# The last down stage of both feed-forward parts as two planned seven-product blocks, with the next norm's work in the plan

## The chip, the cores and the metric

The kernel runs on one core of a Trainium2 chip. The metric is the device time of one execution in microseconds, the median of the runs shown. The profile is one further execution, taken by the hardware profiler.

## The reference

One decoder layer of width 2048 for 256 tokens, in float32: a half-step SwiGLU feed-forward (FFN1), a mixer, a second half-step feed-forward (FFN2), and a final RMS norm.

```python
D_MODEL = 2048; SEQ = 256; D_FF = 5632; FFN_RESIDUAL_SCALE = 0.5

def rms_norm(x, gain):
    var = jnp.mean(x * x, axis=-1, keepdims=True)
    return x * lax.rsqrt(var + NORM_EPS) * gain

def swiglu_ffn(x, w_gate, w_up, w_down):
    return (jax.nn.silu(x @ w_gate) * (x @ w_up)) @ w_down

x = x + 0.5 * swiglu_ffn(rms_norm(x, ffn1_norm), ffn1_w_gate, ffn1_w_up, ffn1_w_down)
z = rms_norm(x, mix_norm) @ w_in          # mixer: a linear recurrence and a short convolution
...
x = x + y @ w_out
x = x + 0.5 * swiglu_ffn(rms_norm(x, ffn2_norm), ffn2_w_gate, ffn2_w_up, ffn2_w_down)
out = rms_norm(x, final_norm)
```

## The kernel before

**Tiles.** The tokens lie in two groups of 128 (t = 0, 1), the model's width in four columns of 512 (c = 0 to 3, `CW` = 512), and the 5632 hidden numbers in 11 units of 512. A matrix product is made in three passes from high and low parts: ScalarE (ACT) casts a weight piece to fp32r (`hi_...`), VectorE (DVE) subtracts to get the rest (`lo_...`), and TensorE (PE) adds high by high, low by high and high by low. One product of a unit (128 tokens, 512 hidden numbers, 512 columns) is therefore 12 matmuls of 512 columns: eight rows that read `hi_d` and four that read `lo_d`. The hidden units are turned (transposed on PE, `ph`) and split the same way into `h`.

**Seven-product blocks.** Two units, two columns and two token groups would take eight products. A block of Strassen's kind makes them with seven, p0 to p6, from sums of weight pieces (made by DVE, or by a transfer on the POOL queue that adds to what lies in memory) and sums of hidden units (`hs`). Its four PSUM banks are `ps_d..._a`, `c`, `d` and `e`; bank a ends as the result of group 1 and d as that of group 0 in one column, e and c in the other. Further units go into the same banks as plain products, x00 to x11: x, unit, column (each is two products, one for each t). With two further units a block has 7 + 8 = 15 products.

**Stages.** Each feed-forward has three down stages: units 0 to 2 in the first, 3 to 6 in the middle, 7 to 10 in the last. The middle stage is laid out by `down_stage` with a `Plan`: steps with an engine, a length, the steps they need and a due time. `run` lists them in the order of a small simulation, and that order is kept on the chip. It makes two blocks, on columns 2 and 1 and then 3 and 0, with p and x items in the order of `down_orders`; the turning of the units still open comes behind the block's p4. What the second block owes to the residual `xres` is handed to the next stage.

The first and the last stage are written out by hand in `down(last)`, and the tile framework's scheduler orders their instructions. Both take column 0 by plain products, columns 1 and 2 by `seven` and column 3 by plain products. With four units that is 8 + 15 + 8 = 31 products. In the first stage the block is on the last two units (`us[-2:]`), since ACT has kept exact copies of those (`turned`, made by `exact` when `again` is set); column 0 takes unit 0, then 2, then 1. Unit 1 is turned last.

**The next norm.** `after(c, t)` is called whenever the last stage has updated a column. For FFN1 it is `to_mixer`: squares for the mixer's norm, and `Norm.later(c)` turns the column; columns 0 to 2 are turned in the stage and column 3 in the mixer's first products. For FFN2 it is `last`, with the final norm's squares and gains. `finish` and `close` end the kernel: the group t = 0 is closed first, then t = 1 in two halves of 256 columns with a bank of their own each (`ps_..._last`); `close` squares, takes the root, scales and stores.

## Time and the profile before

| | |
|---|---|
| time, three runs | 1724.46 us median (1724.23 to 1725.42) |
| the profiled execution | 1725.39 us, of which the span is 1723.6 us |
| TensorE's mean granted clock | 0.998 of full speed |
| PE, DVE, ACT busy | 1708.0, 1527.3 and 1097.9 us |
| FFN1's middle and last down stage | 366.77 to 450.48 and 613.95 to 702.16 |
| FFN2's middle and last down stage | 1380.37 to 1464.10 and 1627.54 to 1715.40 |

Starts and lengths in a row of the timeline are in microseconds from the span's start, and then come the engine, the line, the operation, the tile written and those read, the shape and the count; square brackets give the idle time ahead and what ended it. All rows have line 43, since a wrapper records every operation; they are told apart by their tiles.

### The profile page before, as it was taken

How to read it: one execution, taken by the hardware profiler on the slowest of the kernel's cores; microseconds unless marked ns; L12 is line 12 of the kernel's file. 1: busy time of each engine (PE TensorE's matmuls, PEld its weight loads, DVE VectorE, ACT ScalarE, POOL GpSimd, SP SyncE). 2: the span in 40 equal slices, each digit the busy share in tenths (PEclk: the TensorE clock that was granted, in tenths of full speed). 3: DMA queues.
4: the chain of work that ended last, by engine and by line, in shares of the span. 5: the costliest groups of instructions: out<-in, count | busy, mean ns of one | idle time of the engine just before them, and what ended most of it. 6: DMA issues, size and time to landing. Idle time of an engine off the chain costs nothing.

```text
span 1723.6 us, 20401 instructions
## 1 busy us (share of the span) xinstructions
PE 1708.0 (99%) x7913; PEld 1421.1 (82%) x7913; DVE 1527.3 (89%) x1314; ACT 1097.9 (64%) x1348; POOL 50.8 (3%) x84
## 2 busy tenths in 40 slices
PE   9999999999999999999999999999999999999998
PEld 8888888888888888888888888788888888888876
DVE  7989999998999987887897888789899998999976
ACT  7666576665666655667876656566666665666654
POOL 0010000000000000000000000000000000000000
PEclk9999999999999999999999999999999999999999
DMA  8766777769876865755556675675777778877653
GB/s 284 235 215 219 249 233 234 236 207 266 271 226 226 270 194 182 234 182 185 171 196 212 203 253 155 193 248 169 239 262 226 256 244 249 267 226 237 231 182 122
DMA packets 182450, 383.10 MB, mean 222 GB/s; under 512 B 7508, under 2 KB 10448, under 8 KB 177872
## 3 DMA queue, kind: packets, MB, share of 16 engines
q1 hardware_dynamic: 174656, 340.81, 56.4%
q0 software_dynamic: 7520, 39.92, 11.9%
q8 instruction: 62, 1.02, 0.2%
q10 hardware_dynamic: 176, 1.06, 0.1%
q14 instruction: 36, 0.29, 0.1%
HBM read 339.82 MB, written 2.10 MB: 198 GB/s over the span
## 4 chain that ended last, share of the span: by engine, by line
PE 95%; DVE 2%; ACT 1%; DMA 1%; issue 1%; DVEq 0%; ACTq 0%
PE ps_in L43 10%; PE ps_u_a L43 10%; PE ps_g_a L43 10%; PE ps_d L43 9%; PE ps_d_a L43 7%; PE ps_u_c L43 6%; PE ps_g_c L43 6%; PE ps_u_d L43 4%; PE ps_d_c L43 4%; PE ps_g_d L43 4%; PE ps_d_d L43 3%; PE ps_d_e L43 3%; PE ps_u_e L43 3%; PE ps_o L43 3%; PE ps_g_e L43 3%; PE ps_g L43 2%
## 5 line engine op out<-in xcount | busy, mean ns | idle before, releaser
L43 ACT CAST hi_g_p<-raw_g_w 128x1024 fp32r<-128x1024 f32 (+1 forms) x112 | 139.2, 1263 | 93.6 <-DVE raw_g_w L43 31.9
L43 ACT CAST hi_u_p<-raw_u_w 128x1024 fp32r<-128x1024 f32 x112 | 138.2, 1262 | 65.5 <-PE ps_u_a L43 19.3
L43 DVE TENSOR_TENSOR lo_g_p<-raw_g_w,hi_g_p 128x2560 fp32r<-128x2560 f32 (+2 forms) x72 | 159.9, 2228 | 15.1 <-ACT hi_g_p L43 8.9
L43 DVE TENSOR_TENSOR lo_u_p<-raw_u_w,hi_u_p 128x2560 fp32r<-128x2560 f32 (+2 forms) x72 | 159.1, 2228 | 9.1 <-ACT hi_u_p L43 6.6
L43 PE MATMUL ps_in<-xT_nm,hi_in 128*128 128x512 f32 x512 | 122.5, 391 | 0.0
L43 PEld LDWEIGHTS ps_in<-xT_nm,hi_in 128*128 128x128 f32 x512 | 94.1, 188 | 18.8 <-ACT tha L43 0.5
L43 PE MATMUL ps_d<-hi_d,h 128*128 128x512 f32 x440 | 105.4, 391 | 0.0
L43 PEld LDWEIGHTS ps_d<-hi_d,h 128*128 128x128 f32 x440 | 82.0, 188 | 16.8
L43 DVE TENSOR_TENSOR lo_in<-raw_in,hi_in 128x2048 fp32r<-128x2048 f32 x32 | 73.3, 2290 | 20.7 <-ACT hi_in L43 20.4
L43 ACT CAST hi_in<-raw_in 128x1024 fp32r<-128x1024 f32 x64 | 64.2, 1048 | 33.6 <-PE ps_in L43 18.4
L43 ACT CAST hi_d<-raw_d 128x1024 fp32r<-128x1024 f32 x56 | 55.5, 1047 | 39.3 <-PE ps_d_d L43 11.5
L43 ACT CAST hi_d_p<-raw_d_w 128x1024 fp32r<-128x1024 f32 x56 | 56.1, 1047 | 32.2 <-DVE raw_d_w L43 15.8
L43 ACT CAST hi_d_p<-raw_d 128x1024 fp32r<-128x1024 f32 x56 | 56.5, 1046 | 29.3 <-DVE raw_d L43 16.2
L43 DVE TENSOR_TENSOR lo_d_p<-raw_d,hi_d_p 128x2048 fp32r<-128x2048 f32 x28 | 63.6, 2288 | 11.3 <-ACT hi_d_p L43 11.0
L43 DVE TENSOR_TENSOR raw_u_w<-raw_u_w,raw_u_w 128x1024 f32<-128x1024 f32 (+2 forms) x40 | 69.4, 1756 | 2.8 <-DMA raw_u_w<-in_ffn_w_up_dram 1.8
L43 DVE TENSOR_TENSOR raw_g_w<-raw_g_w,raw_g_w 128x1024 f32<-128x1024 f32 (+2 forms) x40 | 69.5, 1754 | 0.6
L43 DVE TENSOR_TENSOR lo_d<-raw_d,hi_d 128x2048 fp32r<-128x2048 f32 x28 | 63.6, 2288 | 6.8 <-ACT hi_d L43 6.8
L43 DVE TENSOR_TENSOR lo_d_p<-raw_d_w,hi_d_p 128x2048 fp32r<-128x2048 f32 (+1 forms) x36 | 64.8, 1813 | 4.1 <-ACT hi_d_p L43 4.0
L43 PEld LDWEIGHTS ps_in<-xT_nm,lo_in 128*128 128x128 f32 x512 | 65.6, 191 | 2.5
L43 PE MATMUL ps_in<-xT_nm,lo_in 128*128 128x256 f32 x512 | 66.4, 283 | 0.0
L43 DVE TENSOR_TENSOR lo_g_x<-raw_g_x,hi_g_x 128x1536 fp32r<-128x1536 f32 x32 | 56.1, 1754 | 4.6 <-ACT hi_g_x L43 4.6
L43 PE MATMUL ps_u_a<-hi_u_p,x 128*128 128x512 f32 x224 | 57.1, 391 | 0.0
(525 smaller groups left out, 4250.9 us busy)
## 6 DMA issues: line engine op xcount, KB each, us to landing
raw_d<-in_ffn_w_down_dram SPq DMA_DIRECT2D x56, 1024.0 KB, 5.2
raw_g_w<-in_ffn_w_gate_dram SPq DMA_DIRECT2D x32, 1024.0 KB, 6.7
raw_u_w<-in_ffn_w_up_dram SPq DMA_DIRECT2D x32, 1024.0 KB, 6.5
raw_in<-in_w_in_dram SPq DMA_DIRECT2D x32, 1024.0 KB, 5.0
raw_g_x<-in_ffn_w_gate_dram SPq DMA_DIRECT2D x32, 768.0 KB, 7.7
raw_u_x<-in_ffn_w_up_dram SPq DMA_DIRECT2D x32, 768.0 KB, 8.6
raw_u<-in_ffn_w_up_dram SPq DMA_DIRECT2D x23, 1024.0 KB, 6.0
raw_g<-in_ffn_w_gate_dram SPq DMA_DIRECT2D x22, 1024.0 KB, 5.2
```

Source lines behind the costliest of these rows:

```text
L43: ins = getattr(self.engine, name)(*args, **kwargs)
```

## The change

Both last stages become calls of `down_stage`. The stage makes two blocks (columns 1 and 0, then 3 and 2), 30 products instead of 31, and every column's updates are steps of the plan, followed by `after`. In FFN1 the squares and the turning of columns 1 and 0 ("n1", "n0") are steps behind p4 of the second block; columns 2 and 3 are turned in the mixer's first products (`defer`). In FFN2 the final norm's squares and gains are steps, and the last product (p1, group 0) is made in two halves of 256 columns in a bank of their own; `finish` closes group 1 first, then group 0 in halves.

`down` is left to the first stage. No exact copies are made by ACT; the block takes units 0 and 1 (m, n), whose exact values DVE sums from the high and low parts (`v`), and column 0 takes units 0, 1, 2 in turn. In each feed-forward the order has 12 fewer 512-column matmuls. DVE's order has 40 more operations of 512 or 1024 elements a partition and 8 fewer of 2048; ACT has 12 more casts of 1024 and POOL 6 more transfers.

```diff
-            def down(last):
-                us = sorted(set(hidden) | {w[0] for w in waiting})
-                m, n = us[-2:] if turned else us[:2]
-                rest = [u for u in us if u not in (m, n)]
+            def down():
+                m, n, *rest = sorted(set(hidden) | {w[0] for w in waiting})
...
-                        wd, c, rest + [n, m] if turned else [m, n] + rest[::-1], hidden.get, f"d{tag}_{m}_{c}", end,
+                        wd, c, [m, n] + rest, hidden.get, f"d{tag}_{m}_{c}", False,
...
-                def exact():
-                    if again:
-                        act.copy(quad(h), pt)
-                        turned[u, t] = quad(h)
...
-                        for u in () if turned else (m, n):
+                        sh, v = {}, {}
+                        for u in (m, n):
                             for t in range(NT):
-                                turned[u, t] = quad(keep(f"hv{tag}_{u}_{t}"))
+                                v[u, t] = quad(keep(f"hv{tag}_{u}_{t}"))
                                 hi, lo = (f32(hidden[u][:, :, o + t * P : o + (t + 1) * P]) for o in (0, S))
-                                dve.tensor_tensor(turned[u, t], hi, lo, op=ALU.add)
+                                dve.tensor_tensor(v[u, t], hi, lo, op=ALU.add)
...
+                    if final is not None and key == units_only[-1]:
+                        def halves(u=u, q=q):
+                            hi, lo = u.tiles["hi"], u.tiles["lo"]
+                            for o in (slice(0, CW // 2), slice(CW // 2, CW)):
+                                final.append(bank(f"ps_{name}_last")[:, : CW // 2])
+                                parts = [(hi[:, j, o], lo[:, j, o]) for j in range(UK)]
+                                multiply([(final[-1], sf[q], True, True)], parts)
...
             down_orders = (
-                ["p0", "p4", "x01", "x11", "p5", "p1", "p6", "x00", "p3", "x10", "p2"],
-                ["p0", "p4", "x01", "p2", "p5", "x11", "p6", "p1", "p3", "x00", "x10"],
...
+                (
+                    ["p0", "p4", "T", "x01", "x11", "p5", "p1", "p6", "x00", "p2", "p3", "x10"],
+                    ["p0", "p4", "n1", "n0", "x01", "p2", "p5", "x11", "p6", "x00", "x10", "p3", "p1"],
+                ),
+                (
+                    ["p0", "p4", "T", "x01", "x11", "p5", "p1", "p6", "x00", "p2", "p3", "x10"],
+                    ["p0", "p4", "p2", "x01", "p5", "x11", "p6", "x00", "p3", "x10", "p1"],
+                ),
...
+                pairs_of = ((CW, 0), (3 * CW, 2 * CW)) if end else ((2 * CW, CW), (3 * CW, 0))
...
-                    down(True)
+                    final = [] if tag == 2 else None
+                    done, _ = down_stage(s + 1, free, ready, tails, later, final)
+                    if tag == 2:
+                        finish(keep, final)
...
+    def to_mixer(plan, c, t=None, z=None):
...
+            plan.add("ACT", 0.65, lambda: nm.squares(c, (t,)), z, due=40.0)
...
+                turn_into(pt, [xres[:, t, i * P : (i + 1) * P] for i in (k, k + 1) for t in range(NT)])
...
+            a = plan.add("PE", 0.45, turn, *held[c])
...
+                b = plan.add("ACT", 0.41, lambda i=i, parts=parts: parts[i][0](), a, due=5.0)
+                plan.add("DVE", 0.42, lambda i=i, parts=parts: parts[i][1](), b, due=8.0)
...
+        squared = plan.add("ACT", 0.65, square, z, due=10.0)
+        plan.add("DVE", 0.65, lambda: dve.scalar_tensor_tensor(xr, xr, -0.5, fin[:, cs], op0=ALU.mult, op1=ALU.mult), squared, due=25.0)
...
+    def finish(keep, halves):
+        y = [keep(f"y_{t}") for t in range(NT)]
+        Engine.pinned = True
+        close(1, y[1], 0, 1)
+        w = CW // 2
+        for h in range(2):
+            xh = xres[:, 0, D - CW + h * w : D - CW + (h + 1) * w]
+            dve.scalar_tensor_tensor(xh, halves[h], 0.5, xh, op0=ALU.mult, op1=ALU.add)
+            close(0, y[0], h, 2)
```

Three places in the order of instructions show what moves. In a row stand the operation, the tile written, those read, the shape and the count. The first place is PE in FFN1's first down stage, behind column 0's products of unit 0; `ph1_1` are the transposes of unit 1, `h1_2` is unit 2, and `ps_d1_1_0_...` is column 0. Before:

```order
L43 MATMUL ph1_1_1_1222<-ident_71,z1_0_844 128x128 x4
L43 MATMUL ph1_1_0_1230<-ident_71,s1_g1_0_625 128x128 x4
L43 MATMUL ps_d1_1_0_0_1188<-hi_d1_1_0_2_1240,h1_2_1136 128x512 x8
L43 MATMUL ps_d1_1_0_1_1189<-hi_d1_1_0_2_1240,h1_2_1136 128x512 x8
L43 MATMUL ps_d1_1_0_0_1188<-lo_d1_1_0_2_1241,h1_2_1136 128x512 x4
L43 MATMUL ps_d1_1_0_1_1189<-lo_d1_1_0_2_1241,h1_2_1136 128x512 x4
L43 MATMUL ps_d1_1_0_0_1188<-hi_d1_1_0_1_1271,h1_1_1221 128x512 x8
```

After, where `ps_d1_0_0_...` is column 0 and `ps_d1_0_a` the bank of p0 of the block:

```order
L43 MATMUL ph1_1_1_1220<-ident_71,z1_0_844 128x128 x4
L43 MATMUL ph1_1_0_1227<-ident_71,s1_g1_0_625 128x128 x4
L43 MATMUL ps_d1_0_a_1322<-hi_d1_0_p0_1338,h1_0_954 128x512 x3
L43 MATMUL ps_d1_0_0_1_1187<-hi_d1_0_0_1_1236,h1_1_1219 128x512
L43 MATMUL ps_d1_0_a_1322<-hi_d1_0_p0_1338,h1_0_954 128x512 x2
L43 MATMUL ps_d1_0_0_0_1186<-hi_d1_0_0_1_1236,h1_1_1219 128x512
L43 MATMUL ps_d1_0_a_1322<-hi_d1_0_p0_1338,h1_0_954 128x512 x3
L43 MATMUL ps_d1_0_a_1322<-lo_d1_0_p0_1339,h1_0_954 128x512 x3
L43 MATMUL ps_d1_0_0_1_1187<-hi_d1_0_0_1_1236,h1_1_1219 128x512 x3
L43 MATMUL ps_d1_0_0_0_1186<-hi_d1_0_0_1_1236,h1_1_1219 128x512 x7
```

Behind the transposes stood unit 2's 24 matmuls, and unit 1 came after them. Now unit 1 (`h1_1`) comes at once, and matmuls of p0 stand between its first ones; unit 2 comes after unit 1.

The second place is the end of FFN2 on PE; `ps_d2_7_3_0` and `_1` are column 3 of the two token groups, `h2_7` to `h2_10` the units. Before:

```order
L43 MATMUL ps_d2_7_3_0_13244<-hi_d2_7_3_8_13310,h2_8_12098 128x512 x8
L43 MATMUL ps_d2_7_3_0_13244<-lo_d2_7_3_8_13311,h2_8_12098 128x512 x4
L43 MATMUL ps_d2_7_3_0_13244<-hi_d2_7_3_7_13317,h2_7_12271 128x512 x8
L43 MATMUL ps_d2_7_3_0_13244<-lo_d2_7_3_7_13318,h2_7_12271 128x512 x4
L43 MATMUL ps_d2_7_3_1_13245<-hi_d2_7_3_8_13310,h2_8_12098 128x512 x8
L43 MATMUL ps_d2_7_3_1_13245<-lo_d2_7_3_8_13311,h2_8_12098 128x512 x4
L43 MATMUL ps_d2_7_3_last_13358<-hi_d2_7_3_7_13317,h2_7_12271 128x256 x8
L43 MATMUL ps_d2_7_3_last_13358<-lo_d2_7_3_7_13318,h2_7_12271 128x256 x4
L43 MATMUL ps_d2_7_3_last_13371<-hi_d2_7_3_7_13317,h2_7_12271 128x256 x8
L43 MATMUL ps_d2_7_3_last_13371<-lo_d2_7_3_7_13318,h2_7_12271 128x256 x4
```

After, where `ps_d2_4_1_a` is group 1 of column 3 and `_d` group 0:

```order
L43 MATMUL ps_d2_4_1_d_13169<-lo_d2_4_1_x00_13298,h2_10_12804 128x512 x4
L43 MATMUL ps_d2_4_1_a_13133<-lo_d2_4_1_x00_13298,h2_10_12804 128x512 x4
L43 MATMUL ps_d2_4_1_a_13133<-hi_d2_4_1_p3_13296,h2_8_12120 128x512 x8
L43 MATMUL ps_d2_4_1_a_13133<-lo_d2_4_1_p3_13335,h2_8_12120 128x512 x4
L43 MATMUL ps_d2_4_1_a_13133<-hi_d2_4_1_x10_13348,h2_9_12869 128x512 x8
L43 MATMUL ps_d2_4_1_d_13169<-hi_d2_4_1_x10_13348,h2_9_12869 128x512 x8
L43 MATMUL ps_d2_4_1_a_13133<-lo_d2_4_1_x10_13370,h2_9_12869 128x512 x4
L43 MATMUL ps_d2_4_1_d_13169<-lo_d2_4_1_x10_13370,h2_9_12869 128x512 x4
L43 MATMUL ps_d2_4_1_last_13398<-hi_d2_4_1_p1_13324,h2_8_12120 128x256 x8
L43 MATMUL ps_d2_4_1_last_13398<-lo_d2_4_1_p1_13353,h2_8_12120 128x256 x4
L43 MATMUL ps_d2_4_1_last_13411<-hi_d2_4_1_p1_13324,h2_8_12120 128x256 x8
L43 MATMUL ps_d2_4_1_last_13411<-lo_d2_4_1_p1_13353,h2_8_12120 128x256 x4
```

The bank of the group that is closed first (`_3_0` before, `_a` now) was complete 12 matmuls of 512 and 24 of 256 columns ahead of the end. It is now complete 4 of 512 and 24 of 256 columns ahead.

The third place is DVE at the same end; `fin` is the final norm's gain, `y` column 3 times that gain, and `fr` the factor of a group. Before:

```order
L43 SCALAR_TENSOR_TENSOR xres_70<-ps_d2_7_3_0_13244,xres_70 128x512
L43 TENSOR_TENSOR y_0_13384<-xres_70,fin_12908 128x512
L43 RECIPROCAL fy_0_0_13392<-fy_0_0_13392 128x1
L43 SCALAR_TENSOR_TENSOR fv_0_0_13391<-part_0_0_13387,pre_0_13229 128x1
L43 SCALAR_TENSOR_TENSOR fq_0_0_13393<-fv_0_0_13391,fy_0_0_13392 128x1
L43 SCALAR_TENSOR_TENSOR fr_0_0_13394<-fq_0_0_13393,fy_0_0_13392 128x1
L43 TENSOR_SCALAR xres_70<-xres_70,fr_0_0_13394 128x256
L43 TENSOR_SCALAR xres_70<-xres_70,fr_0_0_13394 128x640
L43 TENSOR_SCALAR y_0_13384<-y_0_13384,fr_0_0_13394 128x512
L43 SCALAR_TENSOR_TENSOR xres_70<-ps_d2_7_3_1_13245,xres_70 128x512
L43 SCALAR_TENSOR_TENSOR xres_70<-ps_d2_7_3_last_13358,xres_70 128x256
L43 TENSOR_TENSOR y_1_13385<-xres_70,fin_12908 128x256
```

After:

```order
L43 SCALAR_TENSOR_TENSOR xres_70<-ps_d2_4_1_a_13133,xres_70 128x512
L43 SCALAR_TENSOR_TENSOR xres_70<-ps_d2_4_1_d_13169,xres_70 128x512
L43 TENSOR_TENSOR y_1_13427<-xres_70,fin_12781 128x512
L43 RECIPROCAL fy_1_0_13433<-fy_1_0_13433 128x1
L43 SCALAR_TENSOR_TENSOR fv_1_0_13432<-part_1_0_13428,pre_1_13350 128x1
L43 SCALAR_TENSOR_TENSOR fq_1_0_13434<-fv_1_0_13432,fy_1_0_13433 128x1
L43 SCALAR_TENSOR_TENSOR fr_1_0_13435<-fq_1_0_13434,fy_1_0_13433 128x1
L43 TENSOR_SCALAR xres_70<-xres_70,fr_1_0_13435 128x256
L43 TENSOR_SCALAR xres_70<-xres_70,fr_1_0_13435 128x640
L43 TENSOR_SCALAR y_1_13427<-y_1_13427,fr_1_0_13435 128x512
L43 SCALAR_TENSOR_TENSOR xres_70<-ps_d2_4_1_last_13398,xres_70 128x256
L43 TENSOR_TENSOR y_0_13426<-xres_70,fin_12781 128x256
```

Before, one update of 512 (`ps_d2_7_3_0`) led the closing of the first group, and the other group's update and its first half stood behind it. Now two updates (`_a` for group 1, `_d` for group 0) lead it, and only halves stand behind.

More of the change, by code (lines that the diff above doesn't have):

```diff
@@ L1524, in result @@
                         return
-                    for key in keys:
-                        plan.add("DVE", add_ps, lambda key=key: update(c, t, snaps[key]), made[key], due=9.0)
-                    z = plan.add("DVE", add_ps, lambda: update(c, t, ps()), done, due=6.0)
+                    parts = [plan.add("DVE", add_ps, lambda key=key: update(c, t, snaps[key]), made[key], due=9.0) for key in keys]
+                    z = plan.add("DVE", add_ps, lambda: update(c, t, ps()), done, *(parts if then else ()), due=6.0)
                     if then:
@@ L1650, in down_stage @@
                     sevens(
-                        plan, wd, cols, f"d{tag}_{s}_{i}", sh, rows, xs, rooms, orders[i], pairs[11 * i : 11 * i + 11],
-                        down_result(plan, cols, handed if i else None), fills=fills, down=True,
+                        plan, wd, cols, f"d{tag}_{s}_{i}", sh, rows, xs, rooms, [item(z) for z in down_orders[tag if end else 0][i]],
+                        pairs[11 * i : 11 * i + 11],
+                        down_result(plan, cols, handed if i and not end else None, (lambda c, t, z: after(plan, c, t, z)) if end else None),
+                        fills=fills, down=True, final=final if i else None,
                     )
```

157 lines of the change are left out of this document (78 added, 79 removed).

## The prediction

> **What bounds the kernel now.** I read the page first: the busy times, and the chain of work that ended last.
>
> ```profile
> span 1723.6 us, 20401 instructions
> PE 1708.0 (99%) x7913; PEld 1421.1 (82%) x7913; DVE 1527.3 (89%) x1314; ACT 1097.9 (64%) x1348; POOL 50.8 (3%) x84
> PE 95%; DVE 2%; ACT 1%; DMA 1%; issue 1%; DVEq 0%; ACTq 0%
> ```
>
> TensorE (PE) is busy for 99% of the span and carries 95% of the chain. A matmul taken away is therefore time taken away, unless another engine is then late. VectorE (DVE), at 89%, is the one that could be. Next, the waits of PE in the whole span:
>
> ```profile
> PE ps_d_c L43 <- ACT s_d L43: 1.7, 1, 1.7
> PE ps_d_e L43 <- ACT ps_d_c L43: 1.3, 2, 0.7
> ```
>
> The first of these is in FFN2's last down stage, which the change rewrites. The second is a wait of 0.66 in both middle down stages, whose plan the change takes as its pattern. For the price of a matmul I took the longest run of plain ones from the chain:
>
> ```profile
> 186.78 16.32 PE ps_d L43 x72
> ```
>
> So a 512-column matmul takes 16.32/72 = 0.2267 us, and a product of 12 takes 2.72 us. Last, the four stages in question by windows, which I cut at the first matmul of each stage and at the first of what follows: middle and last of FFN1, then middle and last of FFN2. The columns are the stretch, its length, the busy time of PE, PEld, DVE, ACT and POOL, the granted clock, and the DMA.
>
> ```profile
> 366.77:450.48 83.71, 83.05 (x370) 68.37 (x368) 75.07 (x59) 52.45 (x60) 3.47 (x6) 1.00 0.82 249
> 613.95:702.16 88.21, 88.21 (x405) 73.07 (x404) 70.26 (x60) 55.99 (x85) 1.08 (x6) 1.00 0.57 183
> 1380.37:1464.10 83.73, 83.07 (x370) 68.19 (x369) 75.75 (x61) 52.31 (x60) 4.03 (x6) 1.00 0.81 249
> 1627.54:1715.40 87.86, 86.19 (x393) 71.08 (x391) 67.07 (x62) 46.98 (x66) 0.86 (x1) 1.00 0.46 154
> ```
>
> The middle stage is the new last stage measured: two seven-product blocks, each with 15 products, laid out by the same planner. It takes 83.7 us where the last stages take 88.2 and 87.9. Both clocks are at 1.00, so the difference is work and waits.
>
> **FFN1's last stage.** Before, it had 31 products; now it has 30. The order of instructions has 12 fewer 512-column matmuls in each FFN. The rest of the difference is turning (transposes) and waiting:
>
> ```profile
> 414.97 1.89 PE L43 MATMUL ps_d_e<-hi_d_x,h 128*128 128x512 f32 x7 [0.66 <-ACT ps_d_c L43]
> 677.70 3.79 PE L43 MATMUL ps_d<-hi_d,h 128*128 128x512 f32 x16
> 683.14 1.03 PE L43 MATMUL pt_nm<-ident,xres 128*128 128x128 f32 x8
> 683.93 3.89 PE L43 MATMUL ps_d<-hi_d,h 128*128 128x512 f32 x16
> ```
>
> A group of eight transposes costs 683.93 - 683.14 = 0.79. The sixteen matmuls behind it take 0.1 more than the sixteen at 677.70, which have no turning ahead: I take 0.89. The plan puts the turning of columns 1 and 0 (two such groups) behind p4 of the second block, which is just where the middle stage waits 0.66 for the copies of its banks. So I start from 83.71, take off 0.66 and add 2 x 0.88: 84.8. Before, the stage turned three columns of the next norm and the mixer's opening one; now it is two and two, so 0.89 moves over the border into the mixer. The gain is 88.21 - 84.8 - 0.89 = 2.5. Counted the other way, 12 x 0.2267 = 2.7. I keep 2.5, and 2.2 to 2.8 as its bounds.
>
> **FFN2's last stage.** Here the middle stage is the pattern again, with no turning. The last product is split into two halves of 256 columns. The same split stands at the end of the kernel now:
>
> ```profile
> 1709.64 1.98 PE L43 MATMUL ps_d<-hi_d,h 128*128 128x512 f32 x8
> 1712.36 1.12 PE L43 MATMUL ps_d_last<-hi_d,h 128*128 128x256 f32 x8
> 1714.76 0.64 PE L43 MATMUL ps_d_last<-lo_d,h 128*128 128x256 f32 x4
> ```
>
> Both halves take 1714.76 + 0.64 - 1712.36 = 3.04, which is 0.32 over a whole product. So the stage takes 83.73 + 0.32 = 84.05, and the gain is 87.86 - 84.05 = 3.8. In it is one product (2.7), the wait of 1.7 for the sums of hidden units, which the plan doesn't have, and on the other side the pattern's 0.66 and the 0.32. With a wait of up to 1 us more somewhere, the bound is 2.8; without the 0.66 it is 4.5. What could bring such a wait is DVE's load (a rival below) and the POOL transfers that add weight pieces, 40 instead of 34 in the program:
>
> ```profile
> L43 ACT CAST hi_d_p<-raw_d_w 128x1024 fp32r<-128x1024 f32 x56 | 56.1, 1047 | 32.2 <-DVE raw_d_w L43 15.8
> raw_d_w<-raw_d_w POOLq DMA_DIRECT2D x8, 1024.0 KB, 7.3
> ```
>
> A transfer lands 7.3 after its issue. The closest case is the second block's: one raw tile holds the weights of p4, p5 and p3 in turn, so the transfer for p3 starts when p5's low part is done, before PE comes to p5. From there to p3 stand p5, x11 (two products), p6 and x00 (two): six products, 16.3 us. Less two casts of 1.05 and a low part of 2.29 (its row is below), about 12 are left for 7.3. It is hidden.
>
> **The first down stages.** The seven block is now on units 0 and 1 rather than 1 and 2. Unit 1 is turned last, and is now used at once, where before unit 2's 24 matmuls lay behind the turning. The scheduler fills the gap with eleven matmuls of p0. The rows of FFN1 (ACT's copies of the unit turned first, PE's first matmuls behind the turning of unit 1, ACT's casts, DVE's low parts of p0's weights and of the hidden unit), and then of FFN2:
>
> ```profile
> 137.40 1.19 ACT L43 COPY u_g<-ph 128x512 f32<-128x512 f32 x2 [0.39 <-DVE h L43]
> 145.58 3.91 PE L43 MATMUL ps_d<-hi_d,h 128*128 128x512 f32 x16
> 145.79 1.06 ACT L43 CAST h<-ph 128x512 fp32r<-128x512 f32 x2
> 145.94 2.29 DVE L43 TENSOR_TENSOR lo_d_p<-raw_d,hi_d_p 128x2048 fp32r<-128x2048 f32 x1
> 148.14 1.28 DVE L43 TENSOR_TENSOR h<-ph,h 128x512 fp32r<-128x512 f32 x2
> 1158.87 3.89 PE L43 MATMUL ps_d<-hi_d,h 128*128 128x512 f32 x16
> 1158.72 1.08 ACT L43 CAST h<-ph 128x512 fp32r<-128x512 f32 x2 [0.20 <-PE ph L43]
> 1159.02 2.29 DVE L43 TENSOR_TENSOR lo_d_p<-raw_d,hi_d_p 128x2048 fp32r<-128x2048 f32 x1
> ```
>
> In FFN1, unit 1's first matmul is now the fourth behind the turning, at 145.58 + 3 x 0.2267 = 146.26; the first of the two casts ends at about 146.3, a wait of 0.1 at most. The low part of p0's weights is needed by the eleventh, at 145.58 + 10 x 0.2267 = 147.85, and was there at 145.94 + 2.29 = 148.23. It should come earlier, since ACT no longer makes the copies (1.19) ahead of its casts. In FFN2, unit 1's first matmul is the second behind the turning, at 1159.10, and the first cast ends at about 1159.26: 0.2. The eleventh comes at 1161.14, the low part at 1161.31: 0.2 again, as the casts there come behind a transfer. Unit 1's own low parts are needed 19 matmuls behind the turning, at 149.9, and are there at 149.4. The sums that replace the copies put 4 x 0.6 on DVE, two of them ahead of the turning, where DVE is idle now:
>
> ```profile
> 139.02 0.69 DVE L43 TENSOR_TENSOR s_u<-ps_u_d,s_u 128x512 f32<-128x512 f32 x1 [1.06 <-PE ps_u_d L43]
> 1152.84 0.69 DVE L43 TENSOR_TENSOR s_u<-ps_u_d,s_u 128x512 f32<-128x512 f32 x1 [1.08 <-PE ps_u_d L43]
> ```
>
> The 1.2 us of the two sums fits into those 1.06 and 1.08 and what else is idle there. The cost: 0.1 + 0.4 = 0.5. The bounds: 0, and 3.0 if the sums are not absorbed (148.23 + 1.2 - 147.85 = 1.6 and 1161.31 + 1.2 - 1161.14 = 1.4).
>
> **The tail.** DVE's last rows now:
>
> ```profile
> 1709.84 0.69 DVE L43 SCALAR_TENSOR_TENSOR xres<-ps_d,xres 128x512 f32<-128x512 f32 x1 [4.88 <-PE ps_d L43]
> 1710.57 0.69 DVE L43 TENSOR_TENSOR y<-xres,fin 128x512 f32<-128x512 f32 x1
> 1711.71 0.16 DVE L43 RECIPROCAL fy<-fy 128x1 f32<-128x1 f32 x1 [0.45 <-ACT fy L43]
> 1713.54 0.68 DVE L43 SCALAR_TENSOR_TENSOR xres<-ps_d,xres 128x512 f32<-128x512 f32 x1
> 1714.33 0.42 DVE L43 SCALAR_TENSOR_TENSOR xres<-ps_d_last,xres 128x256 f32<-128x256 f32 x1
> 1715.43 0.42 DVE L43 SCALAR_TENSOR_TENSOR xres<-ps_d_last,xres 128x256 f32<-128x256 f32 x1 [0.21 <-PE ps_d_last L43]
> ```
>
> Call E the end of PE's last matmul, 1715.40 now. The first group of tokens to be closed has its sum 5.76 before E (1709.64), and DVE is free in time for the last half, which it takes at E + 0.03. After the change, the bank of the first closed group (a) is done only 3.95 before E: behind it come 4 matmuls on d (0.91) and the halves (3.04). DVE updates from a at E - 3.75 and from d at E - 2.84 (0.20 behind PE, as 1709.84 is behind 1709.64), multiplies y from E - 2.11, starts the reciprocal at E - 1.38, and 1713.54 - 1711.71 = 1.83 later it comes to the first half: E + 0.45. The second half follows 0.89 later (two steps of 0.42 with their gaps), at E + 1.34. Everything from there to the end is the same. The cost is 1.3. It would be 0.5 if the two updates don't stand in a row, and 1.8 if a step of ACT is in the way.
>
> **The sum.** 2.5 + 3.8 - 0.5 - 1.3 = 4.5 us. The profiled execution took 1725.39 (1.8 around its span), 0.9 above the median; I put the sum on the median: 1724.46 - 4.5 = 1720.0. The rest of the program's order is unchanged.
>
> The Trainium skill, "TensorE: Matmul & The Clock Gate", section "Back-to-back issue gap", gives N/2.4 + 2.5 ns for an isolated matmul of N columns, thus an estimate of 216 ns for 512, and by it the 24 matmuls are worth 5.2 us rather than the row's 24 x 0.2267 = 5.4; its sustained 131 ns would make them 3.1, which the row of 72 contradicts.
>
> **The rivals.**
>
> *Sums not absorbed (0.15).* The unit that is turned late makes PE wait 1.6 and 1.4 in the first down stages. Against it: the idle time above. The gain is then 4.5 + 0.5 - 3.0 = 2.0, the time 1722.5: within the 0.2%. A longer wait would cost more than itself, as the one of 2.68 shows, with the granted clock in the eighth column of its window:
>
> ```profile
> 1110.00:1114.00 4.00, 2.17 (x7) 1.69 (x8) 4.00 (x3) 2.00 (x2) 0.86 (x1) 0.82 0.40 80
> 1111.83 1.49 PE L43 MATMUL ps_u_c<-hi_u_p,xs 128*128 128x512 f32 x4 [2.68 <-ACT hi_u_p L43]
> ...
> 1116.95 1.08 PE L43 MATMUL ps_u_c<-lo_u_p,xs 128*128 128x512 f32 x4
> ```
>
> The 15 matmuls from 1111.83 to 1116.95 took 5.12 instead of 3.40: 1.7 lost to the clock. One such wait would bring the time to about 1724. The same page of the Trainium skill, section "What's actually happening", halves the clock after an idle window of about 3.4 us; here a wait of 2.68 was enough. The stages' windows, with waits of 0.66 and 1.66 in them, stay at 1.00.
>
> *A longer tail or seam (0.10).* The closing chain on DVE, or the mixer's first columns with one more group to turn, gives back 2 more: 1722, within the 0.2%.
>
> *DVE becomes the bound (0.13): the one that ends slower.* In the middle stages DVE is busy 75.07 of 83.71 and 75.75 of 83.73, so 8.6 and 8.0 are idle. On top of the pattern, FFN1's last stage gets eight low parts of 0.42 and two updates of 0.69 (4.7), FFN2's gets six scalings of 0.69, a gain of 0.4 and two updates (5.9): 10.6 in all. DVE works in order, and a low part behind a scaling that waits for ACT's square keeps PE waiting. For it: 81.7 of 84 busy leaves 3% idle. Against it: nothing follows FFN2's last stage, so the low parts that the middle stage makes for its successor (2.29 each) fall away, and the last stages before show 70.26 and 67.07. If nothing is absorbed, the time is 1720.0 + 10.6 = 1730.6. It decides from 4.5 unabsorbed, and is outside the 0.2% from 8. I give 0.10 to that and 0.03 to a part of it that ends near 1724.
>
> *The change doesn't do what it says.* Excluded for the work: the order shows the 24 matmuls gone.
>
> **How the numbers follow.** A measurement of this kernel tells 0.2% (3.4 us) from no change: faster is below 1721.0, slower above 1727.9. My forecast, 1720.0, has 0.62. Its own bounds: with first downs at 0, the tail at 0.5 and 2.7 for FFN1 the gain is 6.0 (1718.4), and runs scatter by 0.5: low 1717.9. The range goes up over the first two rivals, and a small wait with them, to 1723.8. Left out above it are DVE as the bound and the wait that lowers the clock. Faster 0.62, same 0.28 (0.15 + 0.10 + 0.03), slower 0.10.
>
> **What would show it.** Right: FFN1's last stage at 84.8 and FFN2's at 84.1 from first to last matmul, without waits of PE over 0.7 in them; waits under 0.4 behind the turning of unit 1; the second half's update 1.3 behind PE's last matmul, and 9.5 from that matmul to the end of the span instead of 8.2. Wrong: waits of PE for low parts (lo_d) in the last stages, DVE above 95% there; waits over 1 us for h in the first down stages; PE idle at the mixer's first matmuls.

## The result, and the profile after

The changed kernel takes 1719.34 us (median of 7 runs, 1718.1 to 1721.4) where the kernel before takes 1725.12 (median of 7, 1722.83 to 1726.03). The ratio is 0.9970, with a 95% interval from 0.9959 to 0.9982: faster by 5.2 us, 3.1 to 7.1. The forecast was 1720.0, a gain of 4.5.

The first lines of the profile page after, then the five longest rows of PE's waits (total, times, longest):

```profile
span 1718.7 us, 20426 instructions
PE 1702.2 (99%) x7889; PEld 1414.9 (82%) x7889; DVE 1549.4 (90%) x1346; ACT 1110.7 (65%) x1360; POOL 56.1 (3%) x90
PE 96%; DVE 2%; DMA 1%; issue 1%; ACT 1%; DVEq 0%; ACTq 0%
```

```profile
PE ps_u_c L43 <- ACT hi_u_p L43: 2.7, 1, 2.7
PE ps_d_e L43 <- ACT ps_d_c L43: 1.3, 2, 0.7
PE idle L43 <- DVE ones L43: 1.1, 1, 1.1
PE ps_d_c L43 <- ACT ps_d_c L43: 0.7, 1, 0.7
PE ps_u_e L43 <- DVE lo_u_x L43: 0.5, 2, 0.3
```

PE's records are 24 fewer and PE is busy 5.8 us less; DVE is busy 22 us more, and PE is still the chain. The wait of 1.7 for sums of hidden units is gone. In its place stands the pattern's 0.66 in FFN2's new block (`ps_d_c`). The last row is new, and it is in FFN2's second gate and up stage, which the change doesn't touch.

The stages by windows, cut as before: FFN1's last stage, the mixer's start (up to the first matmul of `ps_in_c`), FFN2's second gate and up stage, FFN2's last stage. Then the second and third of these from the kernel before, which were not shown yet:

```profile
612.98:697.49 84.51, 84.51 (x386) 70.15 (x384) 78.81 (x72) 63.93 (x93) 2.92 (x9) 1.00 0.76 224
697.49:722.05 24.56, 24.56 (x150) 21.65 (x148) 19.47 (x26) 15.00 (x23) 0.91 (x8) 1.00 0.85 300
1212.78:1378.21 165.43, 164.56 (x734) 135.05 (x732) 154.12 (x99) 104.87 (x102) 6.51 (x8) 1.00 0.73 234
1625.58:1709.60 84.02, 83.36 (x381) 68.94 (x379) 75.90 (x75) 54.96 (x75) 2.71 (x4) 1.00 0.64 188
```

```profile
702.16:725.64 23.48, 23.48 (x142) 20.90 (x140) 18.12 (x23) 13.38 (x20) 0.92 (x8) 1.00 0.74 269
1216.52:1380.27 163.75, 163.75 (x733) 135.22 (x732) 154.37 (x99) 104.96 (x102) 6.37 (x8) 1.00 0.74 236
```

Both new last stages came out as the middle stage had said: 84.51 and 84.02, at a clock of 1.00. With cuts like these, at the first matmul of each part on PE, the two profiled executions can be laid side by side. "First down" runs from the turning of unit 1 to the block's second product (p4), "its block" from there to the first `ps_g_a` of the next stage.

| stretch (us) | before | after | difference |
|---|---|---|---|
| start to the first 16 `ps_g` matmuls in a row | 20.20 | 18.26 | -1.94 |
| FFN1's first down / its block | 14.53 / 43.63 | 15.13 / 43.78 | +0.60 / +0.15 |
| FFN1's last stage | 88.21 | 84.51 | -3.70 |
| mixer's start | 23.48 | 24.56 | +1.08 |
| FFN2's opening, up to the turning | 141.17 | 140.53 | -0.64 |
| FFN2's first down / its block | 14.50 / 43.94 | 15.10 / 43.78 | +0.60 / -0.16 |
| FFN2's second gate and up stage | 163.75 | 165.43 | +1.68 |
| FFN2's last stage | 87.86 | 84.02 | -3.84 |
| PE's last matmul to the end of the span | 8.2 | 9.1 | +0.9 |

The stretches left out differ by 0.4 in sum. The rows that the change writes anew (first downs, last stages, mixer's start, end) add up to about -4.4. The -1.94 at the start is no part of it: over the fourteen profiles of this document, whose kernels start alike, the start takes 18.1 to 18.5 in seven and 19.9 to 20.3 in the other seven. What differs is the pace of the first matmuls, before and then after:

```profile
5.88 2.08 PE L43 MATMUL ps_g<-hi_g,xT_n 128*128 128x512 f32 x4 [0.21 <-ACT hi_g L43]
5.89 1.20 PE L43 MATMUL ps_g<-hi_g,xT_n 128*128 128x512 f32 x4 [0.51 <-ACT hi_g L43]
```

From the second matmul on they follow each other after 0.43 us in the first row and after 0.23 in the second. The seven late profiles all show the slow pace here, the other seven the fast one.

The end, in DVE's rows after:

```profile
1705.86 0.69 DVE L43 SCALAR_TENSOR_TENSOR xres<-ps_d_a,xres 128x512 f32<-128x512 f32 x1 [2.15 <-PE ps_d_a L43]
1706.77 0.69 DVE L43 SCALAR_TENSOR_TENSOR xres<-ps_d_d,xres 128x512 f32<-128x512 f32 x1 [0.21 <-PE ps_d_d L43]
1707.38 0.68 DVE L43 TENSOR_TENSOR y<-xres,fin 128x512 f32<-128x512 f32 x1
1707.97 0.16 DVE L43 RECIPROCAL fy<-fy 128x1 f32<-128x1 f32 x1
...
1709.80 0.42 DVE L43 SCALAR_TENSOR_TENSOR xres<-ps_d_last,xres 128x256 f32<-128x256 f32 x1
1710.25 0.42 DVE L43 TENSOR_TENSOR y<-xres,fin 128x256 f32<-128x256 f32 x1
1710.59 0.42 DVE L43 SCALAR_TENSOR_TENSOR xres<-ps_d_last,xres 128x256 f32<-128x256 f32 x1
```

PE's last matmul ends at E = 1709.60. The update from a starts at E - 3.74 and that from d at E - 2.83, as worked out. The second half is taken at E + 0.99, without idle time ahead of it: DVE is late with it, not PE.

### The profile page after: what moved, and what is told of

Its sections match the earlier page's. It is cut to its first block, busy times and chain, and to the rows that moved or that the text cites. A ratio compares the mean times of both kernels' runs of the same rounds, so it can differ in the third digit from the quotient of the medians.

```text
span 1718.7 us, 20426 instructions
## 1 busy us (share of the span) xinstructions
PE 1702.2 (99%) x7889; PEld 1414.9 (82%) x7889; DVE 1549.4 (90%) x1346; ACT 1110.7 (65%) x1360; POOL 56.1 (3%) x90
## 3 DMA queue, kind: packets, MB, share of 16 engines
q8 instruction: 62, 1.02, 0.2%
q10 hardware_dynamic: 176, 1.06, 0.1%
## 4 chain that ended last, share of the span: by engine, by line
PE 96%; DVE 2%; DMA 1%; issue 1%; ACT 1%; DVEq 0%; ACTq 0%
PE ps_in L43 10%; PE ps_g_a L43 10%; PE ps_u_a L43 10%; PE ps_d_a L43 9%; PE ps_g_c L43 6%; PE ps_u_c L43 6%; PE ps_d_c L43 5%; PE ps_d_d L43 4%; PE ps_d_e L43 4%; PE ps_u_d L43 4%; PE ps_g_d L43 4%; PE ps_d L43 4%; PE ps_o L43 3%; PE ps_g L43 3%; PE ps_u L43 3%; PE ps_g_e L43 3%
## 5 line engine op out<-in xcount | busy, mean ns | idle before, releaser
L43 ACT CAST hi_d_p<-raw_d_w 128x1024 fp32r<-128x1024 f32 x112 | 112.7, 1048 | 54.5 <-DVE raw_d_w L43 23.0
L43 DVE TENSOR_TENSOR lo_d_p<-raw_d_w,hi_d_p 128x2048 fp32r<-128x2048 f32 (+1 forms) x72 | 129.4, 1812 | 5.8 <-ACT hi_d_p L43 5.5
L43 ACT CAST hi_d_x<-raw_d_x 128x1024 fp32r<-128x1024 f32 x64 | 64.3, 1048 | 18.8 <-PE ps_d_c L43 8.3
L43 DVE TENSOR_TENSOR lo_d_x<-raw_d_x,hi_d_x 128x2048 fp32r<-128x2048 f32 x32 | 72.6, 2286 | 1.4 <-ACT hi_d_x L43 1.4
L43 ACT CAST hi_g_x<-raw_g_x 128x1536 fp32r<-128x1536 f32 x32 | 47.2, 1476 | 14.8 <-DMA raw_g_x<-in_ffn_w_gate_dram 11.1
L43 PE MATMUL ps_g_a<-hi_g_p,x 128*128 128x512 f32 x224 | 56.6, 389 | 0.0
L43 DVE TENSOR_TENSOR lo_u_x<-raw_u_x,hi_u_x 128x1536 fp32r<-128x1536 f32 x32 | 56.1, 1752 | 0.0
L43 ACT CAST hi_u_x<-raw_u_x 128x1536 fp32r<-128x1536 f32 x32 | 47.2, 1476 | 12.6 <-PE ps_u_c L43 7.0
```

Of the source, the lines that this page charges most:

```text
L43: ins = getattr(self.engine, name)(*args, **kwargs)
```

## The experiments

Stretches are read from each run's own profiled execution, with the same cuts. The times of two single executions are not set against each other, since the start scatters by 2 us and FFN2's opening by 4; stretches are.

**The parts one by one.** The first kernel has the new first down stages with the old last stages; the second and third have in addition one of the two new last stages each.

```diff
 # e1: both last stages as before; e2: only FFN2's; e3: only FFN1's
-                    done, _ = down_stage(s + 1, free, ready, tails, later, final)
+                    down_last()      # the function down(True) of before
```

> Only the two first down stages are changed (block on units 0 and 1, exact values by DVE's sums, column 0 in the order 0, 1, 2); both last stages are as before. Theory (the late-turned unit costs little): 1.2 us slower than before, 0.6 in each first down stage, of which the profile shows about 0.6 between the turning of unit 1 and the 35th 512-column matmul behind it. Rival (the sums are not absorbed): 3.0 us slower. Rival (nothing is late): no difference, and the 35 matmuls take 35 x 0.2267 = 7.9 us.

> The changed kernel with FFN2's last stage and the closing as before. Theory (the stage pays, the mixer takes back what is moved): 1.4 us faster than before: FFN1's last stage 3.7 shorter at 84.5, the mixer's start 1.1 longer, the first downs 1.2 longer. Rival (the moved turning exposes a wait at the mixer's start and takes all back): 0 to 1 us slower. FFN2's last stage at 87.9 with its wait of 1.7 for sums.

> The changed kernel with FFN1's last stage and the mixer's start as before. Theory: 1.7 us faster than before: FFN2's last stage 3.8 shorter at 84.0, the end 0.9 longer, the first downs 1.2 longer. Rival (the end gives back more, as the second group's halves stand behind the first group's scaling): under 0.5 us faster. FFN1's last stage at 88.2.

| | ratio to before (95%) | first downs | FFN1's last / mixer's start | FFN2's last / end |
|---|---|---|---|---|
| first downs alone | 1.0010 (1.0001 to 1.0018) | 15.06, 15.13 | 88.16 / 23.48 | 87.90 / 8.2 |
| and FFN1's last stage | 0.9992 (0.9984 to 1.0001) | 16.44, 15.13 | 84.50 / 24.57 | 87.70 / 8.2 |
| and FFN2's last stage | 0.9997 (0.9989 to 1.0006) | 14.98, 15.12 | 88.18 / 23.47 | 84.02 / 9.2 |

FFN1's last stage, the mixer's start, FFN2's last stage and the end follow their own edits within 0.2 us, and nothing else. The first downs alone make the kernel slower, by 1.7 us (0.2 to 3.1), where 1.2 was expected. The second is 1.4 faster (2.8 faster to 0.2 slower), as expected. The third is 0.5 faster (1.9 faster to 1.0 slower) where 1.7 was expected: inside the interval, but not shown by it. For the second and third it is the stretches that speak against the rivals, not the times.

**Where the first downs lose.** Two other orders for them. In the first, the block is on units 1 and 2 and the plain columns 0 and 3 take units 0, 2, 1, as before, with the sums still on DVE. In the second the block stays on units 0 and 1.

```diff
-                m, n, *rest = sorted(...)
+                *rest, m, n = sorted(...)                       # e4 only
-                        wd, c, [m, n] + rest, hidden.get, ...
+                        wd, c, rest + [n, m], hidden.get, ...   # e4
+                        wd, c, [m] + rest + [n], hidden.get, ...  # e6
```

> The changed kernel with the first downs' block on units 1 and 2 and column 0 in the order 0, 2, 1 as before; the exact values are still DVE's sums. Theory (the waits come from using the unit that is turned last at once): the 24 matmuls of unit 2 cover the turning again, 1.0 to 1.2 us faster than the changed kernel, about 6 us faster than before. Rival (the sums on DVE are what is late, now behind the turning of both units): no faster than the changed kernel, with waits for hs in the block of the first down stage.

> The changed kernel with its block on units 0 and 1, but column 0 (and 3) of the first down stages takes the units 0, 2, 1, so that unit 2's 24 matmuls lie behind the turning of unit 1 again. Theory (the first downs lose only by using the late unit at once, and the sums for the block are in time): the stretch from the turning to the block's second product 14.5 us as before, instead of 15.1, in both, and the block no longer than 43.8. Rival (the sums of unit 1 come too late for a block that starts 0.6 earlier, as in the run with the block on units 1 and 2): the block is longer by 0.6 or more.

The block on units 1 and 2 is slower than before: ratio 1.0022 (1.0013 to 1.0031). Its waits of PE in the two first downs, by the timeline:

```profile
167.76 0.96 PE L43 MATMUL ps_d_a<-hi_d_p,hs 128*128 128x512 f32 x3 [2.96 <-ACT s_d L43]
1181.39 0.96 PE L43 MATMUL ps_d_a<-hi_d_p,hs 128*128 128x512 f32 x3 [2.92 <-ACT s_d L43]
```

The stretch from the turning to p4 is back at 14.52 and 14.50, but the blocks take 47.07 and 46.97 instead of 43.78: all four exact sums now come behind the turning, and the sums of hidden units are late by 3 us. My theory for that run fell. Units 0 and 1 belong to DVE's sums, since unit 0's can be made early. With that kept and only the order of column 0 put back, the other run has both: PE behind the turning of unit 1, by the timeline of FFN1,

```profile
144.91 0.60 PE L43 MATMUL ph<-ident,s_g 128*128 128x128 f32 x4
145.27 3.89 PE L43 MATMUL ps_d<-hi_d,h 128*128 128x512 f32 x16
148.99 1.98 PE L43 MATMUL ps_d<-lo_d,h 128*128 128x512 f32 x8
```

The stretches are 14.49 and 14.50, and the blocks 43.67 and 43.66. So 0.6 in each first down is the price of using the unit that is turned last at once. With that order FFN1's first down also hangs on when its weights land. In the ten profiles that have it, it took 14.9 to 16.4, and in step with ACT's wait for the transfer: 14.98 with a wait of 0.23, 15.13 with 0.40 (the changed kernel), 15.39 with 0.64, 15.95 with 1.20, 16.44 with 1.72, and 14.9 in the two that list none. In the four with unit 2 behind the turning it took 14.49 to 14.53, also where the wait was 1.28.

**The end.** Three edits of FFN2's last stage and of the closing.

```diff
 # e7: group 1's scaling on ACT and POOL
-        close(1, y[1], 0, 1)
+        rest = close(1, y[1], 0, 1)
+        rest(((act, 0, 640),))
+        rest(((pool, 640, 1536), (pool, 1536, 2048)))
 # e8: columns 2 and 3 swapped, another order
-                    ["p0", "p4", "p2", "x01", "p5", "x11", "p6", "x00", "p3", "x10", "p1"],
+                    ["p0", "p4", "p1", "x01", "p5", "p6", "x00", "p3", "x10", "x11", "p2"],
 # e9: x10 first high and low on bank a, then on d; d's update behind close(1, ...)
                             u.over(to(b), ...)
+                            if split:
+                                u.under((to(b), ...))
```

> The changed kernel with the scaling of the first closed group taken off DVE: ACT takes its first 640 columns and POOL the other 1408. Theory (the halves' updates are late because they stand behind that scaling on DVE): the second half's update starts 0.1 us behind PE's last matmul instead of 1.0, and the end comes 8.2 to 8.4 behind it instead of 9.1. Rival (it is late by the chain of root and factor, or POOL's scaling becomes the last work): 9.1 or more.

With POOL the second half starts at E + 0.35 instead of 0.99, but the end comes 10.0 behind E: the rival. DVE's and POOL's rows of that run:

```profile
1709.77 1.02 DVE L43 TENSOR_TENSOR y<-xres,fin 128x256 f32<-128x256 f32 x1
1711.16 0.42 DVE L43 TENSOR_TENSOR y<-xres,fin 128x256 f32<-128x256 f32 x1
1712.17 0.56 DVE L43 SCALAR_TENSOR_TENSOR fv<-part,pre 128x1 f32<-128x1 f32 x1
1709.51 2.53 POOL L43 TENSOR_SCALAR xres<-xres,fr 128x896 f32<-128x896 f32 x1 [26.26 <-DVE fr L43]
1712.04 1.55 POOL L43 TENSOR_SCALAR y<-y,fr 128x512 f32<-128x512 f32 x1
```

POOL takes 2.53 and 1.55 us, so group 1's last piece is stored only at 1713.62, and group 0's pieces stand behind it in SP's queue. Its last piece is issued at E + 5.14, where the changed kernel has E + 4.86; the rest of the 0.8 that the end is longer is open. And while POOL works, one of DVE's steps of 256 took 1.02 (0.42 after) and a step of one element 0.56 (0.14), each just behind the start of a step of POOL. The same step for the second half, at 1711.16, took 0.42 with POOL still at work.

> The changed kernel with FFN2's last block turned round: columns 2 and 3 swap their places, p1 comes behind p4 (its bank is ready then), and p2 is the halved last product. Theory (the wait of 0.66 behind p4 is only for the copy of its bank): the wait is gone and FFN2's last stage takes 83.4 instead of 84.0. Rival (p1's weights are needed 16 products earlier, and the loads or DVE are then late): new waits for lo_d_p or hi_d, the stage at 84.0 or more.

Nothing won: 84.06. The wait behind p4 is gone, but p6 now comes right behind p5 on bank a and waits for the copy between them:

```profile
1686.24 2.11 PE L43 MATMUL ps_d_a<-hi_d_p,hs 128*128 128x512 f32 x8 [0.71 <-ACT u_d L43]
```

> The changed kernel with FFN2's last plain product (x10) finished on bank a before it starts on bank d, and group 0's update from d made behind the closing of group 1. Bank a is then complete 5.8 us before PE's last matmul, as before, and not 4.0. Theory (the halves are late because group 1's closing starts late): the second half's update starts 0.0 to 0.1 us behind PE's last matmul instead of 1.0, and the end comes 8.2 to 8.3 behind it instead of 9.1. Rival (the low part of x10 is needed 1.8 us earlier and is late): a wait of PE for lo_d_x and FFN2's last stage longer by as much as the end is shorter.

This was right. PE's rows and DVE's of that run:

```profile
1700.77 1.98 PE L43 MATMUL ps_d_a<-hi_d_x,h 128*128 128x512 f32 x8
1702.58 1.07 PE L43 MATMUL ps_d_a<-lo_d_x,h 128*128 128x512 f32 x4
1703.49 1.98 PE L43 MATMUL ps_d_d<-hi_d_x,h 128*128 128x512 f32 x8
```

```profile
1703.69 0.69 DVE L43 SCALAR_TENSOR_TENSOR xres<-ps_d_a,xres 128x512 f32<-128x512 f32 x1 [0.34 <-PE ps_d_a L43]
1707.39 0.68 DVE L43 SCALAR_TENSOR_TENSOR xres<-ps_d_d,xres 128x512 f32<-128x512 f32 x1
1709.28 0.42 DVE L43 SCALAR_TENSOR_TENSOR xres<-ps_d_last,xres 128x256 f32<-128x256 f32 x1 [0.21 <-PE ps_d_last L43]
```

E is 1709.24 here. Bank a is complete at 1703.49, 5.75 ahead; the second half is taken at E + 0.04 with DVE waiting for PE; the end comes 8.2 behind E, and the stage still takes 83.98 without a new wait in it. So the 0.9 is the late start of group 1's closing, and the update from d that stood in its way; the run moves both, and their shares stay open.

**DVE's slack, and what the turning covers.** Twelve further steps of 0.69 on DVE in FFN2's last stage; and the turning of two columns in FFN1's put behind x01.

```diff
+        for _ in range(2):                                                  # e10, 3 columns of 2 groups
+            plan.add("DVE", 0.65, lambda: dve.scalar_tensor_tensor(xr, xr, 1.0, xr, op0=ALU.mult, op1=ALU.max), squared, due=10.0)
-                    ["p0", "p4", "n1", "n0", "x01", "p2", ...
+                    ["p0", "p4", "x01", "n1", "n0", "p2", ...               # e11
```

> The changed kernel with 12 further operations of 0.69 us on DVE in FFN2's last stage (each gives back its own input), 8.3 us of work placed by the same plan. In the changed kernel DVE is busy 75.9 of 84.0 us there, and about 4 of the 8.1 idle lie in the last 6 us. Theory (DVE is not the bound, but has only some 4 us left): the stage gets 3 to 5 us longer, with waits of PE for low parts. Rival (the order of DVE, and not its load, decides, and there is no slack at all): 8 us longer. Rival (DVE is far from mattering): under 1 us longer.

```profile
1624.81:1712.34 87.53, 84.30 (x381) 68.64 (x379) 82.16 (x83) 54.40 (x74) 2.68 (x4) 1.00 0.61 180
1683.61 1.20 PE L43 MATMUL ps_d_a<-hi_d_p,hs 128*128 128x512 f32 x4 [0.70 <-ACT hi_d_p L43]
1686.92 0.74 PE L43 MATMUL ps_d_a<-lo_d_p,hs 128*128 128x512 f32 x2 [1.65 <-DVE lo_d_p L43]
1710.02 0.68 DVE L43 SCALAR_TENSOR_TENSOR xres<-ps_d_a,xres 128x512 f32<-128x512 f32 x1
```

Of 8.3 us the stage lengthens by 3.5 (87.53 against 84.02), with waits for high and low parts in front of p5 and p6. The end lengthens too, to 10.3 from 9.1: DVE comes to the update from a only at E - 2.32 (E is 1712.34) instead of E - 3.74, with no idle time ahead of it. The other 3.6 found room in idle time.

> The changed kernel with the turning of columns 1 and 0 in FFN1's last stage put behind x01 instead of behind p4. Theory (behind p4 the turning covers the wait of 0.66 for the copies of the banks): that wait comes back, and the stage takes 85.1 to 85.2 instead of 84.5. Rival (the wait is hidden anyway): 84.5.

The stage takes 85.48 instead of 84.51, and the wait is there:

```profile
659.46 1.09 PE L43 MATMUL ps_d_e<-lo_d_p,hs 128*128 128x512 f32 x4
661.21 2.11 PE L43 MATMUL ps_d_e<-hi_d_x,h 128*128 128x512 f32 x8 [0.66 <-ACT ps_d_c L43]
663.17 1.99 PE L43 MATMUL ps_d_c<-hi_d_x,h 128*128 128x512 f32 x8
```

The listed 0.66 costs the stage 0.97. Four matmuls behind 659.46 the next could have started, at 659.46 + 4 x 0.2267 = 660.37, so PE paused for some 0.8; the record of the last matmul, 0.39 long where the next can follow after 0.2267, covers 0.16 of it. The eight matmuls behind the pause then take 663.17 - 661.21 = 1.96 instead of 1.81.

**FFN2's gate and up stage.** It has the same instructions before and after, and was 1.68 longer after. One run set the turn of the weight rooms back to what it had been.

```diff
+                    recent["raw"], recent["pair"] = deque((0, 2, 1)), deque((0, 1))
```

> The changed kernel, but behind FFN1's last stage the turn in which the three raw rooms are given out is set to what it was before (0, 2, 1; the change leaves 2, 1, 0). Theory (the 1.2 to 1.7 us that FFN2's second gate and up stage takes longer in every run with the new FFN1 stage come from the rooms that its loads then get): that stretch, 165.4 us in the changed kernel, falls back to 163.8 to 164.3. Rival (it is a matter of when the transfers fall, not of the rooms): it stays at 165.4 or more.

The stretch is 165.39: the rooms are not the cause. In all eleven profiles with FFN1's new last stage it took 164.97 to 165.59, and in the three with the old one (before, and two of the experiments) 163.75 to 164.26. FFN2's opening goes the other way: 138.0 to 140.5 in the eleven, 140.8 to 142.5 in the three. Part of the opening's scatter is the granted clock: behind a wait in it the clock is halved for 3.41 us in eleven of the fourteen profiles, for 6.83 in one (first downs alone, 142.5), and not at all in two (138.0 and 138.4); each 3.41 loses 1.7. Without that loss the two stretches together take 303.3 to 304.3 in the eleven and 303.2 to 303.4 in the three. DVE's row in the changed kernel shows what is late:

```profile
1266.09 2.82 DVE L43 TENSOR_TENSOR raw_u_w<-raw_u_w,raw_u_w 128x2560 f32<-128x2560 f32 x1 [2.50 <-DMA raw_u_w<-in_ffn_w_up_dram]
```

A weight transfer lands later there: this step starts 53.3 us into the stage, where before it started 51.0 into it. Why it does so is open. The opening wins back a part of what this stretch loses, between the two profiles compared above 0.64 of 1.68.

**Both mends together.**

> The changed kernel with both mends together: column 0 of the first downs in the order 0, 2, 1, and bank a complete early at the end. If they add up as single looks showed (1.2 in the first downs, 0.9 at the end), it is 2.1 us faster than the changed kernel, 6.5 us by the sum of the stretches against before (1718.0 where before is 1724.5), and the stretches are 14.5 and 14.5 from the turnings to the blocks, 84.0 for FFN2's last stage and 8.2 for the end. Rival (the time won comes back as later transfers in FFN2's gate and up stages): 1.0 us or less faster than the changed kernel.

| | ratio to before (95%) | first downs and blocks | FFN2's last / end |
|---|---|---|---|
| the change | 0.9970 (0.9959 to 0.9982) | 15.13 + 43.78, 15.10 + 43.78 | 84.02 / 9.1 |
| with both mends | 0.9963 (0.9950 to 0.9977) | 14.53 + 44.54, 14.49 + 43.69 | 84.02 / 8.2 |

The stretches are as expected, but for FFN1's block, where this execution had a wait for a low part of 0.6 and the run with the order alone had none; ACT's wait for the weights' transfer was 1.28 here and 0.30 there. The median of 6 runs is 1719.24 (1716.29 to 1719.45). Against before it is 6.4 us faster; that it beats the change itself is shown for the stretches (0.6 in FFN2's first down, 0.9 at the end) and not by the times, whose intervals overlap. The 2.1 that was expected against the change is not shown, and the rival (1.0 or less) is not excluded.

## Why the prediction was right

- *What bounds it, and the template.* Right. PE stayed the chain, and the middle stage's 83.7 carried over: 84.51 (worked out: 84.8) and 84.02 (84.05). The runs with one new last stage alone show the same 84.50 and 84.02.
- *FFN1: 2.5.* It was 3.70 - 1.08 = 2.62. The 16 transposes in the plan took 1.66, with 0.11 on the matmuls behind them: 1.77, against 1.76 as worked out. The wait that they cover was worth 0.97 and not 0.66, by the run that moved them, and 83.71 - 0.97 + 1.77 is the 84.51. The mixer took back 1.08 rather than 0.89.
- *FFN2: 3.8.* It was 3.84. The pattern's 0.66 is there, the 1.7 is not, and PE waited for no transfer.
- *First downs: 0.5.* Mis-sized: it was 0.75 + 0.44 = 1.19, inside the bounds. The step that failed is that FFN1's low part of p0's weights "should come earlier, since ACT no longer makes the copies". The time without the copies (1.19, and 0.39 idle ahead of them) went into ACT's casts of the weights standing idle: 1.13 ahead of the first, for which no row gives a cause, and 0.40 ahead of the next, for their transfer. The row of that cast, then the low part, then PE's first matmul of unit 1 and its first ones of the low part:

```profile
137.65 2.95 ACT L43 CAST hi_d<-raw_d 128x1024 fp32r<-128x1024 f32 x3 [0.40 <-DMA raw_d<-in_ffn_w_down_dram]
144.17 2.28 DVE L43 TENSOR_TENSOR lo_d_p<-raw_d,hi_d_p 128x2048 fp32r<-128x2048 f32 x1
144.65 0.49 PE L43 MATMUL ps_d<-hi_d,h 128*128 128x512 f32 x1
146.51 0.96 PE L43 MATMUL ps_d_a<-lo_d_p,h 128*128 128x512 f32 x3
```

  The low part ended at 146.45 and PE took it at 146.51, 0.6 behind the turning's end and ten matmuls, 143.63 + 10 x 0.2267 = 145.90. It came 2.82 behind the turning's end, where before it came 2.65 behind. PE had paused for 0.34 of the 0.6 already in front of unit 1, at 144.65 instead of 143.63 + 3 x 0.2267 = 144.31, since ACT's cast of `h` came behind the same late casts. In FFN2 the forecast added a pause for unit 1 and one for the low part, 0.2 each; they are not a sum, since the first delays PE's need for the second. There too the low part decides:

```profile
1155.18 2.28 DVE L43 TENSOR_TENSOR lo_d_p<-raw_d,hi_d_p 128x2048 fp32r<-128x2048 f32 x1
1157.52 0.97 PE L43 MATMUL ps_d_a<-lo_d_p,h 128*128 128x512 f32 x3
```

  PE took it at 1157.52 and not at 1154.69 + 10 x 0.2267 = 1156.96, so 0.56 late. DVE made it straight behind two other low parts; why those came later against the turning than before is open. No row of waits shows any of these pauses, because the record of a matmul (0.39) covers 0.16 of the pause behind it, and what is left is short; they are seen only by counting matmuls. The sums were absorbed, as said: DVE still had 0.63 idle of the 1.06.
- *The end: 1.3.* It was 0.9. The order of events was right, with the updates at E - 3.74 and E - 2.83; the reciprocal came at E - 1.63 and not at E - 1.38, as y followed its update after 0.61 and the reciprocal y after 0.59, and not 0.73 each, with nothing to wait for. The second half followed the first after 0.79 and not 0.89, so it was at E + 0.99 and not E + 1.34.
- *The sum.* The rewritten parts give about 4.4, forecast 4.5. That it is so close is partly luck: the first downs cost 0.7 more and the end 0.4 less than forecast. The measured 5.2 (3.1 to 7.1) agrees with either. A scatter of 0.5 between runs was too small: seven runs of each kernel lie 3.2 and 3.3 us apart, and the start and the clock can shift one execution by 2 and 1.7 us.
- *The clock.* That a longer wait "would cost more than itself" depends on where the wait falls, and so on the execution. In the fourteen profiles the granted clock changes only at whole multiples of 3.413 us from its other changes. The rows are stretches of that length, cut where the changes fall (the clock is the eighth column): the one that holds the wait of 2.68 in the kernel before and the one behind it, then, in the run with the block on units 1 and 2, the two that share the wait of 2.96 and the one behind them:

```profile
1109.11:1112.53 3.42, 0.74 (x4) 0.62 (x4) 3.42 (x2) 2.45 (x4) 0.86 (x1) 1.00 0.00 0
1112.53:1115.94 3.41, 3.41 (x10) 2.62 (x9) 3.38 (x3) 0.65 (x2) 0.00 (x0) 0.50 1.02 202
163.11:166.52 3.41, 1.69 (x8) 1.06 (x6) 3.41 (x5) 3.41 (x5) 0.00 (x0) 1.00 0.49 185
166.52:169.94 3.42, 2.18 (x9) 1.80 (x10) 3.42 (x4) 2.70 (x5) 0.00 (x0) 1.00 0.41 111
169.94:173.35 3.41, 3.41 (x16) 2.82 (x15) 3.41 (x4) 2.70 (x3) 0.00 (x0) 1.00 0.50 196
```

  The first wait lies in one stretch, and the next runs at half the clock; the second is split between two, and the clock stays. Over all fourteen profiles the clock was halved behind every wait that took 1.87 us or more of one stretch, and behind none that took 1.81 or less. Other executions of that run fared worse: in four of its eleven the mean granted clock was 0.994 or 0.995 and the time 1730.1 to 1731.8, in the other seven 0.996 or 0.997 and 1726.9 to 1728.3. Where in those four it fell is not shown. The Trainium skill, "TensorE: Matmul & The Clock Gate", section "What's actually happening", says that the window in which idleness is counted runs freely and isn't started by the kernel. The rows agree, though no wait here was as long as a whole stretch.
- *The rivals.* Sums not absorbed: no, though the run with the block on units 1 and 2 shows what that costs (3.3 and 3.2 in the blocks, against the change). A longer end or seam: no. DVE as the bound: not at this load, where it was busy 75.90 of 84.02, less than the 81.7 that I had added up, since the stage has no successor to work for; and of 8.3 us more, 3.6 still found room. Its price was right in kind: once the room is used up, PE waits for high and low parts.

## What to carry to other kernels

A stage that a planner has already laid out once in the same program is the best price list for the next: two terms of 84 us came out within 0.3. What a rewritten stage loses is at its seams, so look there for who is turned, summed or closed last and what stands behind it; here 1.2 in the first downs and 0.9 at the end went back that way, and by the stretches reordering a few matmuls got most of it back. A listed wait of PE is shorter than the time it costs (0.66 against 0.97 here), and pauses of 0.3 don't appear at all; count the matmuls between two cuts instead.

## What the runs showed of the hardware that was not expected

- POOL scaled 128x896 floats in 2.53 us, and while it worked DVE's steps of 256 elements and of one took 1.02 and 0.56 us rather than 0.42 and 0.14. The Trainium skill, "GPSIMD Engine Reference", section "1. Specifications", says that POOL shares its SBUF interfaces with DVE and contends with DVE's instructions that have two SBUF inputs, which both of these have. The rows agree only in part, since another such step took its usual 0.42 beside POOL.
- The granted clock falls on a grid of 3.413 us whose place differs between executions: a wait of PE of 2.96 us left it at 1.00, where one of 2.68 elsewhere in the program halved it for 3.41 us.
- The first `ps_g` matmuls, some 6 us into the span, run at half the pace in some executions and at the full pace in others. By the first 16 in a row this has put the execution 2 us behind, whatever the kernel.
